# Six sets of fifteen small loads on the ring of the tile loads, in a group softmax bound by transfers

## The chip, the core and the metric

The kernel runs on one core of a Trainium2 chip. The metric is the time of one execution on the device, in microseconds (us). Before the change the median of three runs was 1326.79 us (1326.12 to 1327.2).

## The reference

The input is `x`, float32, 4 x 4096 x 4352. Each row of 4352 numbers is cut into 8 groups of 544, and a softmax is taken over each group:

```python
x_g = x.reshape(B, N, 8, D // 8)
x_g = x_g - x_g.max(axis=-1, keepdims=True)
exp = np.exp(x_g)
out = exp / exp.sum(axis=-1, keepdims=True)
```

Every number is read once and written once: 285.2 MB in, 285.2 MB out.

## The kernel before

The 16384 rows are cut into 64 tiles of 256 rows. A tile lies in the core's on-chip memory (SBUF) as 128 partitions, each with 2 whole rows, that is 8704 numbers or 34816 B that are contiguous in HBM. It has 16 groups per partition. Six buffers, `bufs[0]` to `bufs[5]`, hold tiles; tile t uses buffer t % 6, and everything is done in place.

The work is written out by hand for each engine, with semaphores between them:

- SyncE (SP) issues the tile loads in order (L100 to L105). From tile 6 on it first waits until the store of tile t - 6 has landed (`stored`, L102), because that tile had the same buffer. The last tile is loaded in two halves (L108), each 128 x 4352. After all loads, SyncE issues the stores of the last two tiles, 62 and 63 (L113).
- VectorE (DVE) takes the negated maximum of each group (L62), and later the reciprocal of the sums (L72) and the product with it (L75). Its order is: the maximum of tile n + 1 first, then reciprocal and scaling of tile n. So the scaling of a tile, and with it the store, stands behind the load of the next tile.
- ScalarE (ACT) computes the exponential of each group with the sum beside it (L86), 16 instructions a tile.
- GpSimd (POOL) waits for the scaling of tile t and issues its store (L117, L118), for tiles 0 to 61. At the end it waits for all stores (L120, L122).

A DMA is issued by an engine into a queue, which has one ring on each of the core's 16 DMA engines. In the profile the loads, and the two stores by SyncE, are queue q1 (hardware_dynamic), the stores by GpSimd are queue q0 (software_dynamic). Each tile transfer puts 8 rows of 34816 B and one 4-byte packet that raises the semaphore on every DMA engine. SyncE issues far ahead: tiles 0 to 5 are issued in the first 4 us.

The last tile's two halves are treated as separate parts by VectorE and ScalarE, so that maximum, exponential and scaling of the first half can start before the second half is there.

Of the kernel before, what the change touches and what calls it, by code (L numbers as in the profile page):

```python
# [1 line left out]

# [4 lines left out]


@with_exitstack
def kernel(  # L10
    ctx: ExitStack,
    tc: tile.TileContext,
    x: bass.AP,
    out: bass.AP,
):
    nc = tc.nc
    G = 8
    P = 128
    R = 2
    NT = 6  # L20
    RG = R * G
    xf = x.flatten_outer_dims()
    of = out.flatten_outer_dims()
    N, D = xf.shape
    Dg = D // G
    nt = N // (P * R)
    LAST = 2
    FIRST = 2
    turns = (nt - 1 - FIRST) // NT
    f32 = mybir.dt.float32  # L30
    X = mybir.AxisListType.X
    Exp = mybir.ActivationFunctionType.Exp
    xt = xf.rearrange("(t p r) d -> t p (r d)", p=P, r=R)
    ot = of.rearrange("(t p r) d -> t p (r d)", p=P, r=R)

    landed = [tc.alloc_semaphore(f"landed{b}") for b in range(NT)]
    stored = [tc.alloc_semaphore(f"stored{b}") for b in range(NT)]
    last_landed = tc.alloc_semaphore("last_landed")
    last_stored = tc.alloc_semaphore("last_stored")


    max_done = tc.alloc_semaphore("max_done")
    exp_done = tc.alloc_semaphore("exp_done")
    rec_done = tc.alloc_semaphore("rec_done")
    scaled = tc.alloc_semaphore("scaled")

    ctx.enter_context(tc.tile_critical(  # L47
        sync_engine=mybir.EngineType.Pool, no_gpsimd_drain=True))
    bufs = [ctx.enter_context(nc.sbuf_tensor(f"xt{b}", [P, R * D], f32)) for b in range(NT)]
    mx = ctx.enter_context(nc.sbuf_tensor("mx", [P, NT, RG], f32))  # L50
    sm = ctx.enter_context(nc.sbuf_tensor("sm", [P, NT, RG], f32))
    rs = ctx.enter_context(nc.sbuf_tensor("rs", [P, NT, RG], f32))

    parts = [(t, slice(0, RG)) for t in range(nt - 1)]
    parts += [(nt - 1, slice(r * G, (r + 1) * G)) for r in range(R)]

    def groups(t, g):
        return bufs[t % NT][:, :].rearrange("p (g d) -> p g d", d=Dg)[:, g, :]

    def vector_max(n):  # L60
        t, g = parts[n]
        i = nc.vector.reduce_max(  # L62
            out=mx[:, t % NT, g], in_=groups(t, g), axis=X, negate=True)
        if g.start == 0:
            i.wait_op(landed[t % NT], 16 * (t // NT + 1), "sem-ge")
        else:
            i.wait_op(last_landed, 16, "sem-ge")
        i.then_inc(max_done, 1)

    def vector_scale(n):  # L70
        t, g = parts[n]
        nc.vector.reciprocal(out=rs[:, t % NT, g], in_=sm[:, t % NT, g]).wait_op(  # L72
            exp_done, n + 1, "sem-ge").then_inc(rec_done, 1)
        xg = groups(t, g)
        nc.vector.tensor_tensor(  # L75
            out=xg,
            in0=xg,
            in1=rs[:, t % NT, g].unsqueeze(2).to_broadcast([P, g.stop - g.start, Dg]),
            op=mybir.AluOpType.mult,
        ).wait_op(rec_done, n + 1, "sem-ge").then_inc(scaled, 1)  # L80

    def scalar_exp(n, count):
        t, gs = parts[n]
        xg = groups(t, gs)
        for g in range(gs.start, gs.stop):
            i = nc.scalar.activation(  # L86
                out=xg[:, g - gs.start, :],
                in_=xg[:, g - gs.start, :],
                func=Exp,
                bias=mx[:, t % NT, g:g + 1],  # L90
                scale=1.0,
                accum_out=sm[:, t % NT, g:g + 1],
            )
            if g == gs.start:
                i.wait_op(max_done, count, "sem-ge")
        i.then_inc(exp_done, 1)

    for t in range(nt):  # L100
        if t >= NT:
            nc.sync.wait_ge(stored[t % NT], 16 * (t // NT))  # L102
        tile_in = bufs[t % NT]
        if t < nt - 1:
            nc.sync.dma_start(out=tile_in[:, :], in_=xt[t]).then_inc(landed[t % NT], 16)  # L105
        else:
            for r in range(R):
                nc.sync.dma_start(  # L108
                    out=tile_in[:, r * D:(r + 1) * D], in_=xt[t, :, r * D:(r + 1) * D],
                ).then_inc(landed[t % NT] if r < R - 1 else last_landed, 16)  # L110
    for t in range(nt - LAST, nt):
        nc.sync.wait_ge(scaled, t + 1 if t < nt - 1 else len(parts))
        nc.sync.dma_start(out=ot[t], in_=bufs[t % NT][:, :]).then_inc(last_stored, 16)  # L113


    for t in range(nt - LAST):
        nc.gpsimd.wait_ge(scaled, t + 1)  # L117
        nc.gpsimd.dma_start(out=ot[t], in_=bufs[t % NT][:, :]).then_inc(stored[t % NT], 16)  # L118
    for t in range(nt - NT, nt - LAST):
        nc.gpsimd.wait_ge(stored[t % NT], 16 * (t // NT + 1))  # L120
    nc.gpsimd.drain()
    nc.gpsimd.wait_ge(last_stored, 16 * LAST)  # L122

    nc.scalar.preload_act_table(Exp)  # L124

    for n in range(FIRST):
        scalar_exp(n, n + 1)
    nc.scalar.sem_inc(max_done, -FIRST)
    with nc.scalar.Fori(0, turns):
        for k in range(NT):  # L130
            scalar_exp(FIRST + k, k + 1)
        nc.scalar.sem_inc(max_done, -NT)
    for k, n in enumerate(range(FIRST + turns * NT, len(parts))):
        scalar_exp(n, k + 1)


    vector_max(0)
    for n in range(len(parts)):
        if n + 1 < len(parts):
            vector_max(n + 1)  # L140
        vector_scale(n)


# [1 line left out]
_INS = ['x']  # L145
_OUTS = [((4, 4096, 4352), 'float32')]


# [23 lines left out]
```

## Time and profile before

| | |
|---|---|
| median of 3 runs | 1326.79 us |
| span of the profiled execution (first to last instruction) | 1324.7 us |
| VectorE busy | 1190.0 us, 90% |
| ScalarE busy | 757.4 us, 57% |
| moved by DMA | 570.48 MB, mean 431 GB/s |
| packets on q1 / q0 | 9648 / 8928 |
| one maximum or one scaling of a whole tile | 9.22 us |
| one tile's load, issue to landing | 32.4 us (median) |
| one tile's store, issue to landing | 51.5 us (median) |

The page gives the profiled execution's span and no separate time for it; the median of the runs is 2.1 us above that span, for what lies around it. Busy shares say how long an engine worked; a wait line says for whom it stood idle. A load's "issue to landing" runs from the issuing instruction to the last semaphore update, so it includes the time in which the transfer stands behind older ones.

### The profile page before, as it was taken

The page shows a single profiled execution, that of the slowest core. Times are in us where ns is not written, and L with a number is a line of the kernel's source. Part 1 is how long each engine was busy: PE and PEld are TensorE (multiplying, and loading weights), DVE is VectorE, ACT ScalarE, POOL GpSimd, SP SyncE. Part 2 cuts the span into 40 slices and gives each one's busy share as a digit, 9 for nine tenths or more (in the row PEclk, how much of TensorE's full clock was granted, in tenths as well). Part 3 has the DMA queues.
Part 4 walks back from the last instruction along what each step waited for, and adds up shares of the span by engine and source line. Part 5 has one row for each costly group of instructions (what it writes and reads, how often), then busy time and mean ns, then how long its engine had stood idle before and what let it go on. Part 6 is the DMA issues. An engine that isn't in the chain of part 4 may idle for free.

```text
span 1324.7 us, 2465 instructions
## 1 busy us (share of the span) xinstructions
DVE 1190.0 (90%) x195; ACT 757.4 (57%) x2049; POOL 33.3 (3%) x66
## 2 busy tenths in 40 slices
DVE  5999999988989889898898998988989889898893
ACT  3765566547456465564655646556465474654751
POOL 0000000000000000000000000000000000000000
DMA  9999999999999999999999999999999999999998
GB/s 404 421 434 433 432 432 434 434 432 431 435 435 432 430 434 437 432 432 432 436 434 430 433 435 433 431 433 435 433 433 431 434 436 432 431 432 437 432 432 372
DMA packets 18582, 570.48 MB, mean 431 GB/s; under 512 B 2064, under 2 KB 2064, under 8 KB 2064
## 3 DMA queue, kind: packets, MB, share of 16 engines
q1 hardware_dynamic: 9648, 294.13, 51.5%
q0 software_dynamic: 8928, 276.30, 48.3%
q14 instruction: 6, 0.05, 0.0%
HBM read 285.21 MB, written 285.21 MB: 431 GB/s over the span
## 4 chain that ended last, share of the span: by engine, by line
another core or an unknown queue 69%; DVE 20%; DMA 7%; ACT 1%; SPq 1%; issue 0%; POOLq 0%
DVE xt L75 10%; DVE mx L62 10%; DMA out_dram<-xt 4%; DMA xt<-in_x_dram 3%; ACT xt L86 1%; SPq L105 1%; DVE rs L72 0%; SPq L167 0%; POOLq L47 0%; POOLq L156 0%
## 5 line engine op out<-in xcount | busy, mean ns | idle before, releaser
L86 ACT ACTIVATE xt<-xt,mx 128x544 f32<-128x544 f32 x1024 | 750.1, 734 | 542.4 <-DVE mx L62 542.4
L62 DVE TENSOR_REDUCE mx<-xt 128x16 f32<-128x8704 f32 (+1 forms) x65 | 590.1, 9079 | 110.8 <-DMA xt<-in_x_dram 110.8
L75 DVE TENSOR_TENSOR xt<-xt,rs 128x8704 f32<-128x8704 f32 (+1 forms) x65 | 590.6, 9086 | 2.2
L86 ACT ACTIVATION_READ_ACCUMULATOR xt<-xt,mx 128x1 f32 x1024 | 191.6, 187 | 0.0
L118 POOL DMA_DIRECT2D out_dram<-xt x62 | 33.1, 534 | 1243.5 <-DVE xt L75 1243.5
L72 DVE RECIPROCAL rs<-sm 128x16 f32<-128x16 f32 (+1 forms) x65 | 15.7, 242 | 2.8 <-ACT xt L86 2.8
L124 ACT ACT_TABLE_LOAD x1 | 1.3, 1283 | 0.9 <-PEq L156 0.9
L156 POOL MEMSET const-float32-0.0<- 128x1 f32 x1 | 0.1, 98 | 0.2 <-issue 0.2
L156 POOL MEMSET const-bfloat16-1.0<- 128x1 bf16 x1 | 0.1, 101 | 0.0
L156 POOL MEMSET const-uint8-127<- 128x1 uint8 x1 | 0.1, 99 | 0.0
L156 POOL MEMSET const-float32-1.0<- 128x1 f32 x1 | 0.1, 98 | 0.0
## 6 DMA issues: line engine op xcount, KB each, us to landing
xt<-in_x_dram SPq DMA_DIRECT2D x63, 4352.0 KB, 32.4
out_dram<-xt POOLq DMA_DIRECT2D x62, 4352.0 KB, 51.5
out_dram<-xt SPq DMA_DIRECT2D x2, 4352.0 KB, 20.1
xt<-in_x_dram SPq DMA_DIRECT2D x2, 2176.0 KB, 35.1
```

The lines of the kernel that those rows point to most:

```text
L62: i = nc.vector.reduce_max(out=mx[:, t % NT, g], in_=groups(t, g), axis=X, negate=True)
L72: nc.vector.reciprocal(out=rs[:, t % NT, g], in_=sm[:, t % NT, g]).wait_op(exp_done, n + 1, "sem-ge").then_inc(rec_done, 1)
L75: nc.vector.tensor_tensor(out=xg, in0=xg, in1=rs[:, t % NT, g].unsqueeze(2).to_broadcast([P, g.stop - g.start, Dg]), op=mybir.AluOpType.mu ...
L86: i = nc.scalar.activation(out=xg[:, g - gs.start, :], in_=xg[:, g - gs.start, :], func=Exp, bias=mx[:, t % NT, g:g + 1], scale=1.0, accum ...
L105: nc.sync.dma_start(out=tile_in[:, :], in_=xt[t]).then_inc(landed[t % NT], 16)
L118: nc.gpsimd.dma_start(out=ot[t], in_=bufs[t % NT][:, :]).then_inc(stored[t % NT], 16)
L124: nc.scalar.preload_act_table(Exp)
L156: nc = _bacc.Bacc("TRN2", target_bir_lowering=False, num_devices=1)
```

## The change

A new tensor `marks` of 16 partitions x 180 numbers, and a new semaphore `marked`. After the load of each of the tiles 2, 6, 14, 57, 59 and 62, SyncE issues fifteen more loads: one of 1 row, one of 2 rows, and so on to 15 rows, each row being 8 B (two numbers) from the head of the input's first rows, written to `marks`. They go on the ring of the tile loads, behind the load just issued and ahead of the next one. Nothing reads `marks`. GpSimd waits at the end for all ninety of them. The instructions of VectorE and ScalarE, the order of the tile loads and stores and their waits stay as they were.

```diff
+    marked = tc.alloc_semaphore("marked")
...
+    AFTER = (2, 6, 14, 57, 59, 62)
+    marks = ctx.enter_context(nc.sbuf_tensor("marks", [16, len(AFTER) * 15 * 2], f32))
...
                 nc.sync.dma_start(
                     out=tile_in[:, r * D:(r + 1) * D], in_=xt[t, :, r * D:(r + 1) * D],
                 ).then_inc(landed[t % NT] if r < R - 1 else last_landed, 16)
+        if t in AFTER:
+            for n in range(1, 16):
+                c = (AFTER.index(t) * 15 + n - 1) * 2
+                nc.sync.dma_start(out=marks[:n, c:c + 2], in_=xf[:n, :2]).then_inc(marked, 16)
...
+    nc.gpsimd.wait_ge(marked, 16 * 15 * len(AFTER))
     nc.gpsimd.drain()
     nc.gpsimd.wait_ge(last_stored, 16 * LAST)
```

## The prediction

> **What bounds the kernel now.** I read the page first, then the waits, then the timeline of VectorE late in the run, then the chain of its last 100 us, then the DMA queues.
>
> ```profile
> DVE 1190.0 (90%) x195; ACT 757.4 (57%) x2049; POOL 33.3 (3%) x66
> DMA  9999999999999999999999999999999999999998
> xt<-in_x_dram SPq DMA_DIRECT2D x63, 4352.0 KB, 32.4
> out_dram<-xt POOLq DMA_DIRECT2D x62, 4352.0 KB, 51.5
> ```
> The DMA row is full in every slice: the 16 DMA engines are the bound, VectorE at 90% is second. A tile's load and store move 2 x 4352 KB, and the stores are issued every 20.6 us in the steady part, so one tile transfer takes 10.3 us when it has the engines to itself. A load needs 32.4 us from issue to landing and a store 51.5: both stand in a queue.
>
> ```profile
> DVE mx L62 <- DMA xt<-in_x_dram: 110.8, 51, 13.9
> SPq L105 <- DMA out_dram<-xt: 1201.7, 57, 67.8
> ```
> VectorE waits 13.9 us for the first tile and then about 2 us a tile, for the load; SyncE waits for stores to free buffers.
>
> ```profile
> 1154.42 9.22 DVE L62 TENSOR_REDUCE mx<-xt 128x16 f32<-128x8704 f32 x1 [1.95 <-DMA xt<-in_x_dram]
> 1163.55 0.24 DVE L72 RECIPROCAL rs<-sm 128x16 f32<-128x16 f32 x1
> 1163.83 9.22 DVE L75 TENSOR_TENSOR xt<-xt,rs 128x8704 f32<-128x8704 f32 x1
> 1175.05 9.22 DVE L62 TENSOR_REDUCE mx<-xt 128x16 f32<-128x8704 f32 x1 [1.99 <-DMA xt<-in_x_dram]
> ```
> These are the maxima of tiles 57 and 58. A period is 20.6 us here; without its wait VectorE needs 18.55 us (9.2 + 9.2 and small steps). So after a late load it makes good 2.06 us a tile, no more.
>
> ```profile
> 1224.87 32.64 DMA xt<-in_x_dram
> ...
> 1257.54 9.22 DVE mx L62
> ...
> 1301.05 4.69 DVE xt L75
> ```
> In the chain, tile 62's maximum starts at 1257.54, and from there VectorE works almost without a pause until the last scaling ends at 1305.75 and the last store is issued. The span ends at 1324.7, 19 us later.
>
> ```profile
> q0 software_dynamic: 702, 21.66, 50.1%
> q1 hardware_dynamic: 700, 21.66, 50.1%
> ```
> This is the DMA view of 600 to 700 us. Stores (q0) and loads (q1) get equal shares. The trace's packet records show how: on one engine packets follow without a gap, a row of 34816 B taking 1.285 us, and the two queues alternate strictly, one row each. The 4-byte packet that raises a semaphore takes 9 ns, and it uses up a turn of its own.
>
> **What the Trainium skill says.** "DMA: Bandwidth & Descriptors", section "Queues, rings and completion order", has each engine go round robin between its queues by packets, of some 9 to 17 descriptors; the records agree on the round robin, but here one row is a turn. Its section "Why a DMA increments its semaphore by 16 and not by 1" says that a DMA from SyncE of n rows, n up to 16, runs on n engines, the lowest-numbered, each raising the semaphore; the trace of before has only 128-row transfers (8 rows and one 4-byte packet per engine) and doesn't show this.
>
> **The change part by part.** *Issue.* Fifteen issues cost SyncE 0.33 to 0.62 us each (its loads' durations), 5 to 9 us a set. A load takes about 30 us to land and SyncE waits some 20 us for its next buffer, so no tile load is issued later. GpSimd's wait at the end is for transfers over long before. VectorE, ScalarE and GpSimd keep their work.
>
> *Packets.* By the page, engine e (0 to 14) gets 15 - e rows of 8 B and as many 4-byte packets a set: 30 on engine 0, none on engine 15. The row of 8 B has no duration in the trace. Lower end: like the semaphore packet, 9 ns. Upper end, an estimate from the same page's table "Measured (HBM->SBUF, 128 partitions, SWDGE, issued from GpSimd)": 0.68 us for 4 KB, 8 pieces an engine, 0.085 us each. I take 0.02 us: 0.3 us for fifteen, plus 0.1 for semaphores. The four sets to load 57 make engine 0 late by 0.6 to 5.7 us, taken as 1.5. An engine is never idle before the end, so it keeps this.
>
> *Turns.* This is the real cost. Each small packet takes a turn of the load queue, and the store queue answers with a full row. While up to 30 small packets pass on engine 0, stores run at full rate and the next load stands still, until the marks are through or the store queue is empty; then the rest drains at once. No engine idles: bytes are conserved, loads are put behind stores. A tile is complete when its slowest engine is, so VectorE sees the worst one.
>
> - Behind load 2: it lands at 34 us, the first store is issued at 44.8. No store to give way to: nothing but the packets.
> - Behind load 6 (ends 101.6 on a typical engine): store 2 has 3 to 4 rows left (it ends at 110), and store 3, issued at 100.4, is seldom there before 106 (store 0's first rows came 4.9 to 7.6 us after its issue; I take 6). About 4 rows pass, 5 us; then the marks drain. Load 7 comes about 5 us late (7.6 if store 3 arrives in time). VectorE has 13 us in hand there. But the lag stays: the queues alternate afterwards, and nothing makes the load queue catch up unless the store queue runs empty.
> - Behind load 14: VectorE has nothing in hand and stalls by up to 20 us. It is made good in about ten tiles, inside its 100 us of slack. During the stall the store queue on the marked engines runs empty, loads catch up, and the lag is about 5 us again.
> - Behind load 57: this one is near the end. On a typical engine load 57 ended at 1151.5; then 58 loads were through, and of store 53 7.8 us at half rate were left: 53.6 stores; together 111.6 transfers of 10.28 us. With the lag of 5 us load 57 lands at 1156.5, its maximum starts at 1157; store 56 is issued 18.9 us after that (1154.42 to 1173.35 in before) and its rows come 6 us later, 1181.9. By then 111.6 + 30.4/10.28 = 114.6 transfers are through; 56 are stores (all that there were), so 58.6 are loads. The missing 0.4 at half rate takes 8.7 us: load 58 lands at 1190.6, its maximum starts at 1191.1 instead of 1175.05, 16 us late.
> - Behind 59: VectorE is behind, store 57 comes late, the store queue is empty at about 1206 when these marks arrive, and they drain. Behind 62: the last load comes some 10 us later on engine 0, but VectorE isn't ready for it before 1283 either. Nothing added.
>
> *The end.* From 16 us, four tiles at 2.06 us give back 8.3: tile 62's maximum and with it the last store are 7.7 us late. Of this, some is covered: a transfer alone needs 12.6 us from issue to landing (load 0: issued 0.9, landed 13.5), while the last store of before needed 17.0 (1305.8 to the last packet, 1322.8), because older stores were still moving. So 4.4 us are hidden and 3.3 stay. The packets' 1.5 us come on top (on the engine that is last). Sum: 1324.7 + 3.3 + 1.5 = 1329.5 us of span. The median of the runs is 2.1 us over the span (1326.79 against 1324.7), so 1331.6.
>
> So up to 12.7 us (8.3 + 4.4) by which load 58 is late cost nothing; every further us costs one.
>
> **The rivals.**
> - *The stall is deeper.* If the lag from load 6 is gone by load 57, load 57 lands at 1151.5, store 56 is there at 1177 and 58.1 loads are through; 0.9 at half rate give 1195.5, a maximum 21 us late, 12.7 at the end, 8.3 after the cover: with packets 1337. For it: 40 tiles lie between. Against: the records show the alternation unbroken for hundreds of us.
> - *Not slower.* The cover of 12.7 us decides: if the small packets of a set take eight turns or fewer (the page has packets of many descriptors), or the lag is 9 us, load 58 is late by less, and the DMA engines still end last: 1326.8 to 1329. For it: bytes added are 6 KB of 570 MB. Against: the semaphore packets' own turns.
> - *Small rows are dear.* The trace of before has no such row, so a price outside my bounds can't be excluded: at 0.5 us each, the 60 rows up to load 57 make engine 0 30 us late, about 1355. Against: the small packets that the trace does have, 9 ns each.
> - *Faster*: the engines have no gap between 2 us and their ends at 1319.8 to 1322.8, so at most 2 us could be had from evening these out, 1325.
>
> **How the numbers follow.** Forecast 0.52, deeper stall 0.16, not slower 0.25, dear rows 0.04, faster 0.03. The predicted time is 1331.6; the range takes in the not slower case from its lower end, 1326.5, and the deeper stall with dearer packets, 1340. A measurement of this kernel can tell about 0.2%, 2.65 us, from no change: slower starts at 1329.4. Of the forecast some 0.07 lie under that (a lag of 6 or 7 us at load 6), so slower 0.65, same 0.32, faster 0.03.
>
> **What would show it.** In the profile after: q1 with 1440 packets more; VectorE's wait for load 15 and for load 58 near 15 to 20 us each instead of 2, no waits for some tiles after each; the maximum of tile 62 at about 1265; DMA rate falling below full in the last 10 us. Wrong it is if load 58 isn't late (small packets take no turns), if tile 57 is already many us late (the lag is larger), or if the DMA row has holes in the middle (small rows dear).

## The result and the profile after

The changed kernel takes 1426.75 us (median of 4 runs, 1423.68 to 1426.78) against 1326.66 us in the same round: a ratio of 1.0749, 95% interval 1.0734 to 1.0764. The forecast was 1331.6, at most 1340. The loss is 100 us, some twenty times the forecast one.

The page of the changed kernel (engines, then DMA, then issues with the median us to landing):

```profile
DVE 1190.2 (84%) x195; ACT 757.4 (53%) x2049; POOL 33.3 (2%) x66
...
GB/s 398 424 433 426 434 430 429 429 427 427 422 421 426 423 409 405 400 401 393 387 396 391 392 400 397 389 394 390 393 404 389 395 399 383 398 409 424 383 247 298
...
q1 hardware_dynamic: 11088, 294.14, 49.1%
q0 software_dynamic: 8928, 276.30, 47.4%
...
xt<-in_x_dram SPq DMA_DIRECT2D x63, 4352.0 KB, 45.1
out_dram<-xt POOLq DMA_DIRECT2D x62, 4352.0 KB, 49.0
```

VectorE, ScalarE and GpSimd work as long as before, and q1 has the 1440 packets more that the change makes. What is new is the row of rates: after a good third of the run (15th slice, 500 us) it falls from 430 to about 395 GB/s and stays near that. The last two slices (247, 298) are the end, where the DMA engines ran out of work. The waits say the same: VectorE stood still for loads for 216.7 us instead of 110.8.

```profile
DVE mx L65 <- DMA xt<-in_x_dram: 216.7, 53, 13.9
```

VectorE's timeline of the changed kernel, late in the run (start, duration, and in brackets the wait before it):

```profile
1226.80 9.22 DVE L65 TENSOR_REDUCE mx<-xt 128x16 f32<-128x8704 f32 x1 [4.06 <-DMA xt<-in_x_dram]
...
1249.35 9.22 DVE L65 TENSOR_REDUCE mx<-xt 128x16 f32<-128x8704 f32 x1 [3.90 <-DMA xt<-in_x_dram]
...
1278.95 9.22 DVE L65 TENSOR_REDUCE mx<-xt 128x16 f32<-128x8704 f32 x1 [10.96 <-DMA xt<-in_x_dram]
```

These are the maxima of tiles 56, 57 and 58. A tile takes 22.6 us, not 20.6, in a stretch where no set of marks is near. From such starts of the maxima, each compared with the same tile's start in the kernel before, the loss can be laid out along the run:

| | later than before, us |
|---|---|
| tile 14 (sets behind 2 and 6 passed) | 16.3 |
| tile 22 (set behind 14 passed) | 21.5 |
| tile 57 (35 tiles without a set) | 94.9 |
| tile 62 (sets behind 57, 59) | 106.1 |
| end of the span | 100.3 |

So 73.4 us came where nothing was added, 2.1 us a tile; the late sets cost 11.2, of which the end hid 5.8.

The busy windows of both kernels show that this isn't idle time alone (columns: window, length, busy us of VectorE, ScalarE and GpSimd with counts, clock, DMA share, GB/s). Before:

```profile
850.00:950.00 100.00, 89.95 (x16) 59.07 (x160) 2.66 (x5) 1.00 1.00 433
```

After:

```profile
850.00:950.00 100.00, 83.89 (x15) 55.39 (x151) 2.12 (x4) 1.00 0.98 397
```

The DMA engines are busy 98% of the time and move 8% less: the rows themselves take longer. The packet records between 500 and 1100 us have no row over 1.34 us in the kernel before, and 128 in every 100 us in the changed one.

The records also show the shape of a period. Fifteen DMA engines do six store rows in a run (the sixth takes 1.8 to 2.4 us, and the load row behind it is often slow too), then load and store rows in turn until their eight store rows are done, then five load rows, then nothing for about 0.7 us, of which up to 0.4 us all fifteen together. The sixteenth alternates load and store all the time and never rests. Its load rows take 1.29 us with few exceptions; of its eight store rows in a period three take 1.29 to 1.34 and five 1.45 to 1.96, on average 1.53. Eight of each kind are 22.5 us: it sets the period. Of the 120 rows of marks behind tile 57, 117 pass at 1223.2 to 1223.7 us and three at 1249.0 to 1254.2, two store rows apart: this engine is a full tile behind, and it is the one with three marks a set. A buffer is free only when the last engine has stored it, so the others wait for it.

### The profile page after: what moved, and what is told of

Read it like the earlier page. It is cut to its first block, busy times and chain, and to the rows that moved or that the text cites. A ratio compares the mean times of both kernels' runs of the same rounds, so it can differ in the third digit from the quotient of the medians.

```text
span 1425.0 us, 2555 instructions
## 1 busy us (share of the span) xinstructions
DVE 1190.2 (84%) x195; ACT 757.4 (53%) x2049; POOL 33.3 (2%) x66
## 4 chain that ended last, share of the span: by engine, by line
DMA 59%; DVE 33%; another core or an unknown queue 6%; ACT 1%; issue 0%; SPq 0%; POOLq 0%
DMA xt<-in_x_dram 30%; DMA out_dram<-xt 29%; DVE xt L78 17%; DVE mx L65 16%; ACT xt L89 1%; DVE rs L75 0%; SPq L108 0%; SPq L175 0%; POOLq L48 0%; POOLq L164 0%
## 5 line engine op out<-in xcount | busy, mean ns | idle before, releaser
L65 DVE TENSOR_REDUCE mx<-xt 128x16 f32<-128x8704 f32 (+1 forms) x65 | 590.1, 9079 | 216.7 <-DMA xt<-in_x_dram 216.7
```

What stands on the lines that cost most here:

```text
L65: i = nc.vector.reduce_max(out=mx[:, t % NT, g], in_=groups(t, g), axis=X, negate=True)
```

## The experiments

The period of 22.6 us was not entered in every execution of the same kernel; where there were two executions both times are given, and the trace is of the first. "Spread" is the time from the first to the last of the 16 semaphore packets of one store, in order of landing; "slow rows" are tile rows over 1.34 us in 100 us, taken between 500 and 1100 us; both are from the packet records. "Set 30" is the set of fifteen small loads behind tile 30; "drained at 30" means that SyncE waits once before the load of tile 30 until both queues are nearly empty.

| run | us | us a tile, 40 to 50 | spread at tile 50, us | slow rows |
|---|---|---|---|---|
| before | 1326.66 | 20.6 | 3.0 | 0 |
| after | 1426.75 | 22.6 | 22.6 | 128 |
| sets 2, 6, 14 | 1344.27 | 20.7 | 9.7 | 47 |
| the same, tensor as in after | 1406.63 | 22.7 | 22.7 | 118 |
| sets 57, 59, 62 | 1338.00 | 20.6 | 2.5 | 0 |
| even sets of 16 rows | 1373.31 | 21.0 | 18.6 | 87 |
| set 30 | 1331.87 | 20.5 | 3.7 | 6 |
| set 14 | 1329.84 | 20.6 | 4.1 | 5 |
| set 6 | 1332.85 | 20.6 | 10.4 | 0 |
| set 2 | 1355.08, 1331.78 | 21.1 | 20.5 | 68 |
| sets 6, 14 | 1423.48, 1350.31 | 22.6 | 22.5 | 173 |
| all but set 2 | 1342.54, 1420.58 | 20.6 | 5.9 | 0 |
| all, drained at 30 | 1357.03 | 20.5 | 2.1 | 8 |
| all, drained at 20 | 1360.31, 1358.91 | 20.6 | 2.1 | 0 |
| all, drained at 45 | 1388.61, 1357.85 | 22.7 (tiles 33 to 43) | 2.4 | 173 to 920 us, 27 from 1000 us |
| before, drained at 20 | 1330.33 (10 runs) | 20.6 | 1.9 | 1 |
| uneven by whole rows | 1352.11, 1352.05 | 20.6 | 20.4 | 2 |
| uneven by part rows | 1428.74, 1331.45 | 22.7 | 22.7 | 137 |

**Which sets, and is it the price of the packets?** The first four runs.

```diff
-    AFTER = (2, 6, 14, 57, 59, 62)
+    AFTER = (2, 6, 14)
```

> The sets behind tiles 2, 6 and 14 alone. Skew theory (unequal numbers of turns set the DMA engines apart, and the state feeds on itself: one engine a tile behind, the others empty for part of each period): about 1420 us, the period of a tile grows from 20.6 to 22.6 us by tile 25 as with all six sets. Price theory (each small packet or each set costs time on its own): about half of the loss, 1375 us.

```diff
-    AFTER = (2, 6, 14, 57, 59, 62)
+    AFTER = (57, 59, 62)
```

> The sets behind tiles 57, 59 and 62 alone, in an undisturbed state. By the working of the prediction for a set that meets full store queues (load 58 some 21 us late, 12.7 us at the end, 4.4 covered): 1331 to 1340 us. Skew theory: the same, there is no time left for the slow state to build up. Price theory: about 1375 us.

```diff
-                nc.sync.dma_start(out=marks[:n, c:c + 2], in_=xf[:n, :2]).then_inc(marked, 16)
+                nc.sync.dma_start(out=marks[:, c:c + 2], in_=xf[:16, :2]).then_inc(marked, 16)
```

> Six sets of fifteen loads of 16 rows: every DMA engine gets 15 rows and 15 semaphore packets a set, so the same number of turns. Skew theory: no slow state, 1327 to 1340 us, with stalls behind tiles 14 and 57. Turn theory (loads put behind stores are enough, on however many engines): 1400 us or more. Price theory: at least the 1427 us of the changed kernel, since twice as many rows are moved.

```diff
-    AFTER = (2, 6, 14, 57, 59, 62)
+    AFTER = (30,)
```

> One uneven set behind tile 30 alone. Skew theory: the slow state starts within some ten tiles of it and lasts to the end, about 20 tiles at 2 us more plus some 10 us of stall: 1350 to 1390 us. Price theory: a sixth of the loss, about 1343 us. If single sets are harmless (a state that only several sets build): about 1327 us.

The price theory falls: the even sets carry twice the rows (90 x 16 against 720) and lose 47 us, half of what the changed kernel loses, where this theory had at least 100; and in the changed kernel the 720 rows of 8 B take 9 ns each in the records, 6.6 us over all engines together. The even sets also stay below the 1400 us of the turn theory, though they have a stall of 25.6 us at tile 58 besides. The skew theory didn't hold as written either: the early sets alone missed their 1420, the single set is nearly harmless (5 us), and even sets, which give each engine the same turns, still drift (their spread goes from 1.6 us at tile 10 to 18.6 at tile 50, and the period reaches 23.4 us before tile 55), outside the 1327 to 1340 us expected of them.

The late sets alone came out as worked out for a deep stall, a little deeper. VectorE in that run, tiles 57 and 58:

```profile
1154.51 9.22 DVE L65 TENSOR_REDUCE mx<-xt 128x16 f32<-128x8704 f32 x1 [1.97 <-DMA xt<-in_x_dram]
...
1200.68 9.22 DVE L65 TENSOR_REDUCE mx<-xt 128x16 f32<-128x8704 f32 x1 [27.53 <-DMA xt<-in_x_dram]
```

Tile 58 is 25.6 us later than in the kernel before (1175.05), tile 62 is 17.3 later: 8.3 us are made good in four tiles, as forecast. The span is 1336.2, 11.5 us longer, so the end hid 5.8.

**Single sets, and the same work once more.**

```diff
-    AFTER = (2, 6, 14, 57, 59, 62)
+    AFTER = (14,)
```

> The set behind tile 14 alone. By what the single set behind tile 30 did: one stall of about 25 us at tile 15, made good by tile 30, then a period of 20.6 to 20.8 us: 1327 to 1337 us. If this set alone starts the slow state: over 1390 us.

```diff
-    AFTER = (2, 6, 14, 57, 59, 62)
+    AFTER = (6,)
```

> The set behind tile 6 alone. Lag theory: load 7 late by 15 us or more, no stall over 3 us at VectorE (13 us in hand), then every load some 15 us later for good; time 1330 to 1342 us by the lag at the end less the 4.4 us of cover. If this set alone starts the slow state: over 1390 us.

```diff
-        if t in AFTER:
+        if t in AFTER[:3]:
...
-    nc.gpsimd.wait_ge(marked, 16 * 15 * len(AFTER))
+    nc.gpsimd.wait_ge(marked, 16 * 15 * 3)
```

> As the run with the early sets alone, with the tensor of the marks at the size of the changed kernel: up to tile 57 the work and the addresses are those of the changed kernel. If the state is settled by the work: 22.6 us a tile and about 1420 us. If small differences of timing choose it: anything from 1340 to 1420 us, period other than 22.6.

The times of the sets behind 14 and 6 alone are in their ranges. The set behind tile 6 shows the lasting lag in pure form, at 11 us instead of the 15 expected: tile 14 is 11.3 us late, tile 57 is 11.6, the spread is 10.4 us, and no row between 500 and 1100 us is slow. This lag neither grows nor heals, and costs 6.4 us of span at the end. The last run does the work of the early sets and took 1406.63 where its twin, with a smaller tensor for the marks, took 1344.27. From tile 14 to 30 its spread wanders between 11 and 19 us, it reaches 21 us at tile 33, and from tile 36 on the period is 22.6; the changed kernel, with the same work up to there, has 22 us or more from tile 21 on. So the work does not settle when the state is reached; the spread drifts up to it. The runs with two executions below show that the work does not settle whether it is reached either.

**Is one set the culprit?** The sets behind 2 and without it, two executions each.

> The set behind tile 2 alone, which meets no stores: fifteen small loads on an empty store queue. Set-2 theory (it sets the DMA engines at different points in their rows, and from then on rows collide and take longer): 50 or more rows over 1.34 us in every 100 us from 50 us on, a period of 20.8 us or more, a spread between the first and last engine of a store that grows; 1335 to 1410 us. Turn theory (only sets that meet stores do harm): 1327 us, no slow rows, spread 2 to 4 us.

> The sets behind tiles 6 and 14. Set-2 theory: the lag of the set behind 6 and the stall of the set behind 14, rows of 1.288 us again after some 20 tiles, period 20.6: 1330 to 1340 us. Turn theory: slow state as with the early three, 1340 to 1410 us.

> All sets but the one behind tile 2. Set-2 theory: no 22.6 us period; the lag of the early sets and the stall at tile 58, 1335 to 1350 us, so 75 us or more of the loss gone. Turn theory: 1400 us or more, as with all six.

No. The set behind tile 2 alone met its expectation in one execution, with slow rows and a growing spread (the first tile rows after its marks took 1.5 to 3.1 us), but never reached the 22.6 us in the trace. And the state comes without it: the sets behind 6 and 14 took 1350.31 us once and 1423.48 once; all sets but the one behind 2 took 1342.54 and 1420.58. So no one set is the culprit, and the same program may drift into the state or not.

**Does the state keep itself up?** SyncE waits once until the queues are almost empty, so that all DMA engines start anew together.

```diff
             nc.sync.wait_ge(stored[t % NT], 16 * (t // NT))
+        if t == 45:
+            nc.sync.wait_ge(stored[(t - 2) % NT], 16 * ((t - 2) // NT + 1))
```

> All six sets and the wait for an almost empty DMA queue before the load of tile 45, late enough that the 22.6 us period should be there before it. State theory (the period lasts only because one engine is a tile behind): 22.6 us a tile before tile 45, 20.6 us or less from 46 to 57, spread from 22 us to about 2; some 1420 us, since the wait costs about what it saves by then. If the slow period returns at once after the wait: about 1450 us.

VectorE in this run, tiles 42 to 46:

```profile
896.33 9.22 DVE L65 TENSOR_REDUCE mx<-xt 128x16 f32<-128x8704 f32 x1 [3.67 <-DMA xt<-in_x_dram]
...
919.27 9.22 DVE L65 TENSOR_REDUCE mx<-xt 128x16 f32<-128x8704 f32 x1 [4.30 <-DMA xt<-in_x_dram]
...
939.87 9.22 DVE L65 TENSOR_REDUCE mx<-xt 128x16 f32<-128x8704 f32 x1 [1.95 <-DMA xt<-in_x_dram]
...
984.10 9.22 DVE L65 TENSOR_REDUCE mx<-xt 128x16 f32<-128x8704 f32 x1 [25.59 <-DMA xt<-in_x_dram]
...
1002.66 9.21 DVE L65 TENSOR_REDUCE mx<-xt 128x16 f32<-128x8704 f32 x1
```

and its windows before and after the wait:

```profile
800.00:900.00 100.00, 79.52 (x14) 51.12 (x140) 2.66 (x5) 1.00 0.97 392
...
1060.00:1120.00 60.00, 59.90 (x10) 36.26 (x99) 1.59 (x3) 1.00 1.00 431
```

Before the wait there are 22.9 us from tile 42 to 43 and 392 GB/s; after one stall of 25.6 us the rate is 431 GB/s, VectorE has no wait at all for ten tiles, and the spread has gone from 23 to 2.4 us. The buffers and the work of a tile are the same before and after, so the slowness is a state that depends on what went before, and one restart removes it. The time of 1388.61 us is less than the 1420 expected. The wait at tile 20 and the one at tile 30 come before the state is reached.

> All six sets and a wait of SyncE before the load of tile 20 until the store of tile 18 has landed, so that both queues run nearly empty and the engines start anew. State theory: the spread between the engines falls to about 2 us there, slow rows become rare, the period is 20.6 us to tile 57, and the end loses what the late sets cost: 1340 to 1360 us, 70 us less than without the wait though a wait was added. If the slow rows come from something else than the engines' positions: 1420 us or more.

> All six sets, and before the load of tile 30 SyncE waits until the store of tile 28 has landed, so that both queues run nearly empty once and all DMA engines start anew together. State theory (the 22.6 us period lasts because one engine stays a tile behind the others): the period is 22.6 us before the drain and 20.6 us or less after it up to tile 57; with a single stall of 30 to 50 us about 1400 to 1425 us. If the slowness needs no history (a property of the addresses or of the chip's later work): 22.6 us after the drain too, about 1460 us.

> The kernel before, with only the wait before the load of tile 20. It gives the price of that wait: a stall of some 25 us at VectorE, made good in about 12 tiles; 1330 to 1350 us. With it the loss of the marked kernel with the same wait (33 us) can be parted into wait and late sets.

With the wait at tile 20 the two executions took 1358.91 and 1360.31 us, 67 us less than the changed kernel although a wait was added; the late sets are still in it. In the run drained at 30 the state hadn't been reached by then, so it tells only that the spread fell, from 12.1 (tile 26) to 0.2 us (tile 28). In the kernel before, the wait itself costs 3.9 us (1330.33 against 1326.45). With it the 33.8 us of span that the run drained at 20 still loses can be parted: its tile 57 is 24.3 us late, of which 6.1 are the wait, as in the kernel before with the wait, and 18.2 the early sets; the late sets add 15.4 by tile 62, and the end hides 5.9.

**What makes rows slow: small packets, or unequal positions?** Two kernels without any marks. The loads of tiles 6 and 14 are cut, once by rows, once so that the uneven part is 704 columns only; VectorE's wait counts the pieces.

```diff
+    UNEVEN = (6, 14)
...
-            nc.sync.dma_start(out=tile_in[:, :], in_=xt[t]).then_inc(landed[t % NT], 16)
+            for p, c in pieces(t):
+                nc.sync.dma_start(out=tile_in[p, c], in_=xt[t, p, c]).then_inc(landed[t % NT], 16)
```

with `pieces(t)` for tiles 6 and 14 being, by whole rows, `[(slice(0, 120), slice(0, R * D)), (slice(120, P), slice(0, R * D))]`

> No marks. The loads of tiles 6 and 14 are cut into 120 and 8 partitions, so that (if 120 rows run on 15 engines and 8 rows on 8) one engine is 8 rows short and eight engines have one more, a displacement by whole rows. Position theory, whole rows harmless: rows stay at 1.288 us, 1327 to 1332 us. If any unequal share between the engines starts slow rows: more than 20 rows over 1.34 us in every 100 us after tile 14, a growing spread, 1335 to 1425 us.

and by part rows `[(slice(0, P), slice(0, 8000)), (slice(0, 120), slice(8000, R * D)), (slice(120, P), slice(8000, R * D))]`

> No marks. The loads of tiles 6 and 14 are cut so that only 704 of 8704 columns go unequally over the engines, a displacement by less than a row (up to 0.8 us). Position theory, part rows collide: slow rows and a growing spread as in the marked kernels, 1335 to 1425 us. If small packets and long delays are needed: 1327 us and no slow rows.

Windows of the kernel uneven by whole rows:

```profile
600.00:900.00 300.00, 269.81 (x44) 172.52 (x468) 7.97 (x15) 1.00 1.00 433
```

and of the one uneven by part rows:

```profile
600.00:900.00 300.00, 247.28 (x42) 156.61 (x425) 6.91 (x13) 1.00 0.96 394
```

The second is the changed kernel's state again, 394 GB/s, 22.7 us a tile and 1428.74 us, with no small load in it. So neither the 8 B rows nor long delays are needed. This rests on one execution; the other took 1331.45 us.

The first kernel settles less than it was made for. Its cut loads did run unequally: q1 has 14 packets more than before, which is what 15 + 8 semaphore packets in place of 16 give for two loads. From 600 us on it has a spread of 20.4 us, and yet rows of 1.288 us and a period of 20.6, so an engine that stands a tile apart is not slow by that alone. But by the count of its semaphore packets this engine is a tile ahead of the other fifteen, while in the changed kernel it is a tile behind. And its rows were not harmless while the cut loads ran. The page of this kernel has two dips of the rate with busy engines:

```profile
DMA  9999999999999999999999999999999999999997
GB/s 407 418 363 350 434 435 432 398 335 428 432 434 436 430 432 435 435 431 431 436 433 432 432 435 433 432 433 435 432 432 433 436 431 432 433 435 431 434 425 341
```

Between 80 and 118 us and between 255 and 295 us, around the two cut loads, it moved 295 and 323 GB/s, with most load rows at about 2 us and some up to 4.8. By 300 us it had moved 9.5 MB less than the kernel before, which are 22 us at 433 GB/s, out of the 25.6 us that it loses (tile 57 and tile 62 are both 29.5 us late). So the loss is from the cut loads themselves and not from a lag as behind set 6, and its expectation of 1327 to 1332 was wrong on that. Why the rows of a load cut in this way take longer was not tested.

## Why the prediction was wrong

The step that failed is the sentence under *Turns*: "No engine idles: bytes are conserved, loads are put behind stores", and under it the use of 1.285 us for a row throughout (1.288 on average in the records). Conservation makes a displacement between engines cost nothing until the end. That holds only while every row keeps its time. The trace of before had not one slow row from 300 to 1150 us, and I took that for a property of the transfer. With the marks it did not last: rows of over 1.34 us appeared, up to 2.95, the spread between the engines grew along with them, and the state with 22.6 us a tile followed. By 1250 us the changed kernel had moved 509 MB and the kernel before 540; these 31 MB take 72 us at 433 GB/s. In the run with set 6 alone it was 540 too: there bytes were put off and none lost, as the step has it. 73.4 of the 100 us came between tiles 22 and 57, in this state. No rival had it. The one with dear small rows had looked for a slower packet, but in the marks; they take 9 ns. Of the three signs of being wrong, the second came true: tile 57 was already 94.9 us late.

By its other steps:

- *Issue* and GpSimd's wait: no cost seen. A small load took SyncE 0.24 to 2.2 us to issue, 0.41 in the median.
- *Packets*: 9 ns for a row of 8 B, the lower end. The sum for that end was off: four sets of 30 packets at 9 ns are 1.1 us, not 0.6. The Trainium skill's account in "DMA: Bandwidth & Descriptors", section "Why a DMA increments its semaphore by 16 and not by 1", fits: one engine with exactly three rows of the 120 was seen in each of the last three sets.
- *Behind load 2*: nothing but the packets, it said. This set alone took 1331.78 us in one execution and 1355.08 in the other, where ten of the first tile rows after the marks took 1.5 to 3.1 us and slow rows went on.
- *Turns*, alternation: confirmed. In the records of the run with set 6, each row of marks and each semaphore packet stands between two store rows, and the set gives a lag that stays to the end. It is 11 to 12 us at VectorE against 5 forecast (7.6 if store 3 arrived in time): store 3 was there in time, and the marks went on taking turns until its eight rows were through; only then did the rest drain at once.
- *Behind load 14*: up to 20 us forecast; with this set alone tile 15 is 24.6 us late (313.79 against 289.19). It is made good to 6 us by tile 26, in about ten tiles as forecast; the rest stays.
- *Behind load 57*: 16 us forecast for load 58, 25.6 with the late sets alone. The rival with the deeper stall had 21.
- *The end*: 2.06 us a tile made good, as forecast; the cover was 5.8 us, not 4.4.
- Without the state the sum would probably have been too low all the same: all sets but the one behind 2 took 1342.54 us when they missed it, 11 us over the forecast and just over the range.

## What stays open

Why rows take longer once the engines are displaced was not settled, nor that displacement is what starts it: even sets drifted too. The kernel cut by parts of a row reached the state in one execution of two, the one cut by whole rows in none of two. So few executions can't tell these two apart, and the idea that streams collide at some distances and not at others was not tested; no run measured a collision.

Why the engine left behind has slow store rows and normal load rows is not shown either, but the records of the changed kernel have a regularity. In the periods followed between 700 and 910 us, its three store rows that run while all fifteen others store take 1.29 to 1.34 us, and its store rows that run while most of the others load (about 9 to 15 of them) take 1.45 to 1.96. Stores beside loads are not slow by that alone: in the kernel before each engine alternates between them, at 1.288 us a row.

## What to carry to other kernels

Where a kernel sits at the ceiling of the DMA engines, ask of a change not only how many bytes or packets it adds but whether it treats the engines alike: a transfer that not all of them share can displace them, and the slowness that follows can outlast its cause by a thousand us. Equal shares were no safeguard here: the even sets lost 47 us. Compare the rate in stretches far from the change, and the spread between the first and last engine of one transfer; if the rate is low there and the spread is near a whole period, one wait that lets the queues run nearly empty is a cheap test (3.9 us in the kernel before), and here, placed before the state was reached, it saved 67 us. Run such a kernel more than once before you believe one trace.

## What was not expected of the hardware

- Two executions of one program on one core differed by 73 to 97 us (1350 and 1423, 1343 and 1421, 1331 and 1429), while the kernel before varied by less than 3 us.
- A steady period of 22.6 to 22.7 us a tile came up in four kernels with different beginnings, with a spread of 22.5 to 22.7 us at tile 50 (a fifth, drained at 45, came near it before the wait). In the run with sets 6 and 14 the semaphore packets show four engines left behind, in the other three one.
- In the kernel before, the DMA engines kept 1.288 us a row for hundreds of us, and the alternation between the queues was strict to the single row.
